# Projections in pairs of blocks by seven products of sums, one attention over all heads with operands through DRAM, and an output projection in two parts

## The chip, the cores and the metric

The kernel runs on one core of a Trainium2 chip. The metric is the device time of one execution in microseconds; lower is better. A core has TensorE (PE, the matrix engine, with its weight loads as PEld), VectorE (DVE), ScalarE (ACT), GpSimd (POOL) and SyncE (SP, which here issues nearly all DMAs). Each engine, and each engine's DMA queue, takes its own instructions in order; semaphores order the engines among each other. SBUF is the on-chip memory with 128 partitions, PSUM the accumulators of TensorE, DRAM the device memory.

## The reference

One layer of a hybrid backbone. The latent x is 1024 tokens (a grid of 16 rows of 64 columns) by 1024 features, the context 256 tokens by 1024. Both are normalised and modulated to h; one projection w_in (1024 x 3840) feeds a short convolution, an attention over 8 heads of 64 features, and a Conformer convolution; each result is gated, and one output projection is added to x.

```python
PROJ_SIZES = [W_SC] * 4 + [W_NA] * 4 + [W_CF] * 3      # 4 x 256, 4 x 512, 3 x 256 columns
...
def short_conv_branch(z_h, z_b, z_c, z_g, w_conv):
    return z_b * dwconv(z_c * z_h, w_conv) * jax.nn.silu(z_g)
...
def conformer_branch(z_p, z_q, z_g, w_conv, b_conv, ln_g, ln_b):
    u = z_p * jax.nn.sigmoid(z_q)
    u = dwconv(u, w_conv) + b_conv.astype(u.dtype)
    u = layernorm(u, ln_g, ln_b)
    return jax.nn.silu(u) * jax.nn.silu(z_g)
...
    s_win = jnp.einsum('bqhd,brqchd->bhqrc', qr, kw).astype(jnp.float32) * scale + bias[None]
    s_ctx = jnp.einsum('bqhd,bkhd->bhqk', qr, kc).astype(jnp.float32) * scale
    s = jnp.concatenate([s_win.reshape(b, h, GRID_W, kr * NA_COLS), s_ctx], axis=-1)
    p = jax.nn.softmax(s, axis=-1).astype(v.dtype)
```

A query of the attention sees a window of 8 rows by 16 columns of the grid, with a learned bias, and all 256 context keys. The Conformer's convolution has 31 taps on 256 channels, the short one 3 taps.

## The kernel before, in words

**Arithmetic.** A float32 product is made of two parts each, hi and lo (fp32r): three matmuls, h_hi·w_hi, h_lo·w_hi and h_hi·w_lo, which `mm_k` (L324 to L326) issues for one k of 128 input features. `split` (L129, L130) makes the parts: ACT copies, and VectorE or GpSimd subtracts. h lies in SBUF with features on partitions, in `h_lat` (hi and lo, 8 k by 1024 tokens) and `h_ctx`.

**Projection.** w_in is 30 blocks of 128 columns. A block's weights come by two DMAs (`wr`, two buffers) and are split, the low part on GpSimd. 26 blocks give features on partitions: for each half of 512 tokens 8 k by three matmuls into one PSUM buffer of `ps_z` (three buffers), which a sink then reads. The values' four blocks are projected together with tokens on partitions by `v_proj`, 10 tiles of 128 tokens by 8 k by three (L412 to L414), and stored to DRAM (`vd`). The keys of the context add 8 k by three matmuls of 256 columns per pair of heads.

**Stages.** `start` norms x and the context, computes the modulation and projects the first pair's queries and keys; its order is written out in the table SEQ for VectorE, ACT, GpSimd and SP. Then come `cf_in(0)`, the context keys of pair 0, `v_proj`, and the gate of pair 0. Four times `attend` runs a pair of heads: 16 blocks of 128 queries, and between them 48 units of projection (one unit is one k, three matmuls) from an iterator of what is left (`MF`, three units a block). An attention block is `scores` (PE into the one buffer of `ps_s`; VectorE adds the bias and takes the minimum, ACT exponentiates, GpSimd scales), two blocks later `transposed` (PE into the one buffer of `ps_t`; ACT and VectorE split), then `values` into `po` and `fold`. Queries come through `qd` DMAs out of SBUF (`q_parts`, L359), values through `vt` from DRAM (`v_load`, L435), the bias tables of the next head by 21 DMAs (L502). After attention the output projection `out_mm` (8 tiles of tokens by 2 halves by 8 channels by 3) runs as a stage of its own, with the gate multiplied on VectorE (`out_part`).

**Order.** On PE the program's own order holds. Helpers keep a clock of PE work (`pe`), and `spawn`, `poll` and `yield` insert the other coroutines by it: the 62 operations of the 31-tap convolution (L685, 1024 columns on VectorE), `ada_gates`, the bias set-up. Behind the start stage a scheduler orders the other engines, so their instructions stand where their inputs let them.

Of the kernel before, what the change touches and what calls it, by code (L numbers as in the profile page):

```python
# [16 lines left out]
P = 128  # L17
# [20 lines left out]
MF = (3, 3, 3, 3)  # L38
# [3 lines left out]
R_CF, R_CFB, R_LNG, R_LNB, R_SC = 0, 62, 64, 66, 68  # L42

# [13 lines left out]
b4 B30 m4 g4 v4 b5 B31 g5 v5 R3 m5 C3 n4 a6 f6 u6 a7 f7 u7 q80 n5 b6 g6 v6 q90 m6 b7 g7 v7 r82 m7 x8 n6 x9  # L57
O Q00 c0 c1 h0 o0 h1 o1 Q01 n7 c2 c3 h2 o2 h3 o3 Q02 Q10 Q11 Q12
# [7 lines left out]
class Builder:  # L66
# [237 lines left out]
    def load_w(self, src):  # L304
        return [w for g in range(2) for w in self.split_w(self.load_wraw(src, g))]
# [7 lines left out]
    def split_w(self, wr):  # L313
# [3 lines left out]
        self.split(wh, wl, wr, self.nc.gpsimd)  # L317
        return [(wh[:, i], wl[:, i]) for i in range(hk)]
# [27 lines left out]
    def sink_q(self, half, ps):  # L346
# [4 lines left out]
        hi, lo = (self.qn[:, i].rearrange("p b (r c) -> p r b c", c=BW)[:, rows] for i in range(2))  # L351
# [3 lines left out]
    def q_parts(self, h, bg):  # L355

        q = self.qp.tile([P, 2, 4, P], F32R, name="qd")
        for d in range(2):
            self.nc.sync.dma_start(out=f32(q[64 * d:64 * d + 64]),  # L359
                                   in_=f32(self.qn[64 * h:64 * h + 64, :, 4 * bg:4 * bg + 4]))  # L360
# [13 lines left out]

    def sink_gate(self, half, ps):
        sl = slice(half * HALF, (half + 1) * HALF)
        self.silu2(self.sg[:, sl], ps)
# [9 lines left out]
    def v_weights(self, pool):  # L387
        self.wv = wh, wl = [pool.tile([P, KT, HALF], F32R, name=f"wv{i}") for i in range(2)]
        raw = [self.t4.tile([P, T], F32, name="acc") for _ in range(2)]
        raw.append(self.t4.tile([P, T + NTAP - 1], F32, name="t4", tag="t4")[:, 0:T])  # L390
        raw.append(self.t2.tile([P, T], F32, name="yb", bufs=1))
        k = 0
        todo = []
        for t in raw:
            n = t.shape[1] // HALF
            t = t.rearrange("p (k n) -> p k n", n=HALF)
            src = self.a["w_in"][k * P:(k + n) * P, 2048:2048 + HALF].rearrange("(k p) n -> p k n", p=P)
            self.nc.sync.dma_start(out=t, in_=src)
# [793 lines left out]
```

## Time and profile before

| what | us |
|---|---|
| runs of the kernel before | 617.97 and 619.17, median 618.57 |
| the profiled execution's own time | 617.89 |
| its span in the trace | 616.1 |
| TensorE busy in it | 593.8 |
| VectorE, ACT, GpSimd busy | 401.1, 244.0, 178.4 |

In the profile a row of a group is: line of the kernel, engine, operation, output tile <- input tiles, shapes, number of instructions, then busy time and mean duration in ns, then the idle time before them and what ended it. A row of the timeline begins with start and duration in us. A row of the windows has, for a stretch of the span, the busy time and number of instructions of each engine, the clock granted to TensorE, the share of time in which the DMA engines were busy, and their rate. SPq rows are DMAs as SP issues them.

### The profile page before, as it was taken

The numbers are of one execution on the slowest core, as the hardware profiler recorded it, in microseconds if no ns is written. First come the engines' busy times: TensorE is split into PE (matmuls) and PEld (weight loads), VectorE is DVE, ScalarE is ACT, GpSimd is POOL, SyncE is SP. The second block draws the span as 40 slices with busy tenths as digits, with TensorE's granted clock in tenths as the row PEclk, the third lists the DMA queues.
The fourth block names the chain that finished last, engine by engine and source line by source line (L and its number), as shares of the span: only waits on it lengthen the run. The fifth ranks groups of instructions, "written<-read, shape, count | busy, mean of one in ns | idle before, by whom it ended". The sixth has DMA issues, their size and how long they took to land.

```text
span 616.1 us, 8935 instructions
## 1 busy us (share of the span) xinstructions
PE 593.8 (96%) x3101; PEld 497.0 (81%) x3101; DVE 401.1 (65%) x682; ACT 244.0 (40%) x468; POOL 178.4 (29%) x199
## 2 busy tenths in 40 slices
PE   7799999899999999999999999999999999999995
PEld 5467887688888888888888888888788888888884
DVE  4466977798356589577797666836879456352433
ACT  2455812111255542455523554424645434331222
POOL 1231112300233221424322433313434270265112
PEclk9999999899999999999999999999999999999998
DMA  8991658965623117331146242172311455770122
GB/s 286 357 326 41 222 151 175 158 173 160 164 49 93 37 55 202 75 86 49 28 136 141 48 113 55 36 222 52 82 28 35 133 151 160 273 272 1 70 102 103
DMA packets 97171, 78.64 MB, mean 128 GB/s; under 512 B 26508, under 2 KB 80870, under 8 KB 96998
## 3 DMA queue, kind: packets, MB, share of 16 engines
q1 hardware_dynamic: 95397, 71.51, 41.6%
q10 hardware_dynamic: 1728, 6.55, 3.0%
q8 instruction: 25, 0.41, 0.3%
q14 instruction: 21, 0.16, 0.1%
HBM read 55.93 MB, written 14.29 MB: 114 GB/s over the span
## 4 chain that ended last, share of the span: by engine, by line
PE 82%; DVE 6%; DMA 4%; ACT 2%; issue 2%; SPq 1%; POOL 1%; DVEq 0%; POOLq 0%; ACTq 0%
PE ps_z L324 13%; PE ps_z L326 13%; PE ps_z L325 13%; PE po L620 5%; PE ps_t L608 5%; PE ps_f L868 5%; PE ps_f L869 5%; PE ps_f L867 5%; PE ps_s L589 4%; DMA t<-in_w_ada 2%; PE ps_s L590 2%; PE ps_z L412 2%; PE ps_z L414 2%; PE ps_z L413 2%; DMA wa<-in_w_ada 2%
## 5 line engine op out<-in xcount | busy, mean ns | idle before, releaser
L324 PE MATMUL ps_z<-h,wh 128*128 128x512 f32 x384 | 151.1, 394 | 0.0
L326 PE MATMUL ps_z<-h,wl 128*128 128x512 f32 x384 | 150.2, 391 | 0.0
L325 PE MATMUL ps_z<-h,wh 128*128 128x512 f32 x384 | 149.7, 390 | 0.0
L130 POOL TENSOR_TENSOR wl<-wr,wh 128x512 fp32r<-128x512 f32 x52 | 71.8, 1384 | 146.8 <-ACT wh L129 118.0
L599 POOL TENSOR_SCALAR pr<-pr,sm 128x640 f32<-128x640 f32 (+1 forms) x64 | 52.9, 827 | 138.0 <-DVE sm L598 117.2
L326 PEld LDWEIGHTS ps_z<-h,wl 128*128 128x128 f32 x384 | 72.1, 188 | 16.1
L685 DVE SCALAR_TENSOR_TENSOR acc<-t,half_w,acc 128x1024 f32<-128x1024 f32 x60 | 83.0, 1384 | 1.0
L325 PEld LDWEIGHTS ps_z<-h,wh 128*128 128x128 f32 x384 | 72.2, 188 | 12.4
L324 PEld LDWEIGHTS ps_z<-h,wh 128*128 128x128 f32 x384 | 72.2, 188 | 12.1
L612 ACT ACTIVATE pw<-ps_t 128x640 fp32r<-128x640 f32 (+1 forms) x64 | 43.5, 680 | 90.7 <-PE ps_t L608 90.6
L594 DVE CUSTOM_DVE_ANT_0 ps_s<-ps_s,bt 128x640 f32<-128x640 f32 (+1 forms) x64 | 51.0, 796 | 33.7 <-PE ps_s L590 31.0
L613 DVE TENSOR_TENSOR pw<-ps_t,pw 128x640 fp32r<-128x640 f32 (+1 forms) x64 | 50.4, 788 | 17.3 <-ACT pw L612 16.9
L597 ACT ACTIVATE pr<-ps_s,mn 128x640 f32<-128x640 f32 (+1 forms) x64 | 49.0, 766 | 20.2 <-DVE mn L594 19.2
L620 PE MATMUL po<-pw,vt 128*128 128x256 f32 x304 | 51.3, 297 | 2.0 <-DVE yb L571 1.0
L868 PE MATMUL ps_f<-wol,y 128*128 128x512 f32 (+1 forms) x136 | 51.6, 379 | 0.0
L869 PE MATMUL ps_f<-woh,y 128*128 128x512 f32 (+1 forms) x136 | 51.5, 379 | 0.0
L867 PE MATMUL ps_f<-woh,y 128*128 128x512 f32 (+1 forms) x136 | 51.5, 379 | 0.0
L129 ACT ACTIVATE wh<-wr 128x512 fp32r<-128x512 f32 x52 | 32.5, 629 | 34.9 <-PE ps_z L325 20.9
L608 PE MATMUL ps_t<-ident,pr 128*128 128x128 f32 x304 | 43.6, 272 | 0.0
L620 PEld LDWEIGHTS po<-pw,vt 128*128 128x128 f32 x304 | 40.4, 189 | 3.8 <-issue 3.4
L589 PE MATMUL ps_s<-kt,qd 128*128 128x384 f32 (+1 forms) x128 | 42.2, 351 | 0.5 <-ACT pr L597 0.4
L608 PEld LDWEIGHTS ps_t<-ident,pr 128*128 128x128 f32 x304 | 36.0, 142 | 1.8 <-issue 0.9
(171 smaller groups left out, 911.4 us busy)
## 6 DMA issues: line engine op xcount, KB each, us to landing
wr<-in_w_in SPq DMA_DIRECT2D x52, 256.0 KB
wa<-in_w_ada SPq DMA_DIRECT2D x16, 512.0 KB
qd<-qn SPq DMA_DIRECT2D x32, 256.0 KB
vd<-t SPq DMA_DIRECT2D x20, 256.0 KB
x_in<-in_x SPq DMA_DIRECT2D x8, 512.0 KB
t<-in_w_ada SPq DMA_DIRECT2D x16, 256.0 KB
vt<-vd SPq DMA_DIRECT2D x32, 128.0 KB
fraw<-in_w_out SPq DMA_DIRECT2D x8, 512.0 KB
```

Source lines behind the costliest of these rows:

```text
L130: i2 = (eng or nc.vector).tensor_tensor(out=lo, in0=src, in1=f32(hi), op=ALU.subtract)
L324: nc.tensor.matmul(ps, lhsT=wh, rhs=hh, start=(k == 0), stop=False)
L325: nc.tensor.matmul(ps, lhsT=wh, rhs=hl, start=False, stop=False)
L326: self.last = nc.tensor.matmul(ps, lhsT=wl, rhs=hh, start=False, stop=(k == KT - 1))
L589: nc.tensor.matmul(win, lhsT=q[:, b % 4], rhs=kwin, start=(i == 0), stop=(i == 1))
L599: nc.gpsimd.tensor_scalar(out=pr, in0=pr, scalar1=sm, scalar2=0.5, op0=ALU.mult, op1=ALU.mult)
L608: nc.tensor.transpose(out=pt[:, c * P:(c + 1) * P], in_=pr[:, c * P:(c + 1) * P], identity=self.ident)
L620: self.nc.tensor.matmul(po, lhsT=vt[:, vi, h], rhs=pw[:, c], start=(c == 0), stop=(c == n - 1))
L685: self.after_pe(nc.vector.scalar_tensor_tensor(out=acc, in0=u[:, t:t + T], scalar=self.half_w[:, 2 * t + ct:2 * t + ct + 1], in1=acc, op0= ...
L867: nc.tensor.matmul(ps, lhsT=yh, rhs=wh[:, ch], start=(first and i == 0), stop=False)
L868: nc.tensor.matmul(ps, lhsT=yh, rhs=wl[:, ch], start=False, stop=False)
L869: nc.tensor.matmul(ps, lhsT=yl, rhs=wh[:, ch], start=False, stop=(last and i == len(chs) - 1))
```

## The change

1. **Start.** The start stage projects the queries of pairs 0 and 1 (before: queries and keys of pair 0) and stores them to DRAM (`Q`, `Z`). It also loads and splits the first context keys' weights (`Y`, `y`).
2. **Context keys.** `k_ctx` projects the context keys of all four pairs in a row, 96 matmuls of 256 columns, and stores them.
3. **Values and half-sums.** `v_proj` takes its tiles in the order 4 to 7, then 0 to 3, 8, 9. Meanwhile `t_first` and `t_last` build the three sums and one difference of quarters of h that the seven products need (tokens in halves, input features in halves); one quarter is stored to DRAM, overwritten, and loaded again afterwards (`block12`).
4. **Seven products.** `sum_products` projects ten pairs of blocks. Two blocks by two halves of the input features form a 2 x 2 matrix of weights, and two halves of tokens by two halves of features one of h; the 2 x 2 product is made of seven products of sums (the Winograd form of Strassen's) instead of eight: 7 x 4 k x 3 matmuls. `sum_weights` builds the sums of weights on GpSimd and VectorE and splits all seven, six low parts on GpSimd. The results are put together with `snap` (ACT, PSUM to SBUF), `add` (VectorE, onto PSUM) and one addition on GpSimd. The 31-tap convolution runs beside this (`conv_all`, from the third pair on).
5. **Attention in one piece.** `attention` runs over all 64 blocks of eight heads; keys, values, queries and gates are loaded per head from DRAM (`kv_load`, `q_parts`). Between two blocks stand two units of other work: first the last two pairs of blocks in the old form (gates of pairs 2 and 3, the Conformer's gate), then `out_first`, the output projection's part of the convolution channels (0, 1, 6, 7), which adds x and stores the sum to DRAM (`xr`).
6. **Output.** The attention channels (2 to 5) follow after attention, onto `xr`. The gate is multiplied into w_out on GpSimd (`load_wout`) rather than into the results.

The diff, cut to its core:

```diff
-O Q00 c0 c1 h0 o0 h1 o1 Q01 n7 c2 c3 h2 o2 h3 o3 Q02 Q10 Q11 Q12
+O Q00 c0 c1 h0 o0 h1 o1 Q01 n7 c2 c3 y0 h2 o2 h3 o3 y1 Q10 Q11 Z
...
+    def k_ctx(self, w0):
...
+        ws, raw = [w0, split(raws(1))], raws(2)
+        for pair in range(NPAIR):
+            yield from self.proj(ws[pair], T, TC, lambda ps: sink(pair, ps))
+            if pair < 2:
+                ws.append(split(raw))
+                if pair == 0:
+                    raw = raws(3)
...
+    def kv_load(self, hd):
+        pair, h = hd // 2, hd % 2
+        kt = self.slot(h, TA)
+        self.nc.sync.dma_start(out=f32(kt), in_=self.kd_dram[pair][:, h])
+        vt = self.slot(2 + h, (NB + 2) * P).rearrange("p (n e) -> p n e", e=P)
...
+        for b in range(NB):
+            src = bass.AP(tensor=vd.tensor, offset=vd.offset + b * BW * D + c, ap=[[GW * D, 16], [D, BW], [1, P]])
+            dma(out=f32(vt[:, b]), in_=src)
...
+    def sum_weights(self, cols):
...
+        for c0, c1, f in cols:
+            a11, a21, a22 = raw(c0, 0, f), raw(c1, 0, f), raw(c1, 1, f)
+            yield parts(a11)
+            s1 = op(G, a21, a22, ALU.add)
+            s3 = op(V, a11, a21, ALU.subtract, a21)
+            yield parts(s3)
+            s2 = op(G, s1, a11, ALU.subtract)
+            a12 = raw(c0, 1, f)
+            yield parts(s2)
+            yield parts(a12)
+            s4 = op(V, a12, s2, ALU.subtract, s2)
+            yield parts(s1)
+            yield parts(s4, V)
+            yield parts(a22)
...
+            for m in (1, 7, 6, 2, 5, 3, 4):
+                wh, wl = todo.popleft()
+                todo.extend(itertools.islice(ws, 1))
+                chain = m in (1, 6, 5)
+                ps = s if chain else self.ps_z.tile([P, HALF], F32, name="ps_z", tag="z")
+                for i in range(KT // 2):
...
+                if m == 1:
+                    s1 = snap(s)
+                elif m == 7:
+                    s7 = snap(ps)
+                elif m == 6:
+                    s2 = snap(s)
+                    nc.gpsimd.tensor_tensor(out=s2, in0=s2, in1=s7, op=ALU.add)
+                elif m == 2:
+                    add(ps, s1)
+                    sink(0, 0, ps)
+                elif m == 5:
+                    s4 = snap(s)
+                    add(s, s7)
+                    sink(1, 1, s)
+                elif m == 3:
+                    add(ps, s4)
+                    sink(0, 1, ps)
+                else:
+                    add(ps, s2, ALU.subtract)
+                    sink(1, 0, ps)
...
+                self.spawn(self.conv_all(2.1))
...
+                if b == 4 and hd < 7:
+                    kv[hd + 1] = self.kv_load(hd + 1)
...
+        next(steps)
+        while go(fill, 2):
+            next(steps)
...
+            nc.gpsimd.tensor_tensor(out=raw, in0=raw, in1=self.gates[half].unsqueeze(1).to_broadcast([P, 2, HALF]),
+                                    op=ALU.mult)
```

How the order moves, at three places. The first is TensorE at the end of the start stage. In the names, `ps_z` is a PSUM buffer, `h_78` and `h_79` (after: `hc_106`, `hc_107`) the hi and lo parts of h of the latent (after: of the context). Before:

```order
L1012 MATMUL po<-h_79,wh 128x512
L279 MATMUL ps_h<-ident,x_in 128x128 x8
L146 MATMUL ps_a<-ident,rows 128x74
L324 MATMUL ps_z<-h_78,wh 128x512
L325 MATMUL ps_z<-h_79,wh 128x512
L326 MATMUL ps_z<-h_78,wl 128x512
```

After:

```order
L1201 MATMUL po<-h_100,wh 128x512
L280 MATMUL ps_h<-ident,x_in 128x128 x8
L147 MATMUL ps_a<-ident,rows 128x74
L325 MATMUL ps_z<-hc_106,wh 128x256
L326 MATMUL ps_z<-hc_107,wh 128x256
L327 MATMUL ps_z<-hc_106,wl 128x256
```

The start stage is followed by the context keys' 256-column matmuls, 24 for each pair's weights, where a block of 512-column matmuls stood.

The second is VectorE beside the convolution (`acc`). Before, in `v_proj`, it alternates with the split of the values (`t`):

```order
L424 TENSOR_TENSOR t_1149<-ps_z,t_1149 128x4x64
L685 SCALAR_TENSOR_TENSOR acc<-t_734,half_w,acc 128x1024
L424 TENSOR_TENSOR t_1153<-ps_z,t_1153 128x4x64
L685 SCALAR_TENSOR_TENSOR acc<-t_734,half_w,acc 128x1024 x2
L424 TENSOR_TENSOR t_1187<-ps_z,t_1187 128x4x64
```

After, in a job of seven products, with sums of weights (`wq`), a low part (`wl`), the adds onto PSUM (`ps_z`, `ps_s`) and the sink of queries or keys (`st_hcb`):

```order
L377 TENSOR_TENSOR st_hcb<-ps_z,st_hcb 64x8x8x8
L524 TENSOR_TENSOR wq<-wq 128x512
L872 SCALAR_TENSOR_TENSOR acc<-t_1403,half_w,acc 128x1024
L131 TENSOR_TENSOR wl<-wq,wh 128x512
L872 SCALAR_TENSOR_TENSOR acc<-t_1403,half_w,acc 128x1024
L524 TENSOR_TENSOR wq<-wq 128x512
L872 SCALAR_TENSOR_TENSOR acc<-t_1403,half_w,acc 128x1024
L564 TENSOR_TENSOR ps_z<-snap,ps_z 128x512
L872 SCALAR_TENSOR_TENSOR acc<-t_1403,half_w,acc 128x1024 x2
L564 TENSOR_TENSOR ps_s<-snap,ps_s 128x512
L564 TENSOR_TENSOR ps_z<-snap,ps_z 128x512
```

The adds, which free PSUM for TensorE, stand behind one or two convolution steps each. GpSimd in the same jobs, where before it had only the low parts of weights, after:

```order
L586 TENSOR_TENSOR snap<-snap 128x512
L131 TENSOR_TENSOR wl<-wq,wh 128x512 x2
L524 TENSOR_TENSOR wq<-wq 128x512
L131 TENSOR_TENSOR wl<-wq,wh 128x512 x3
L524 TENSOR_TENSOR wq<-wq 128x512
```

It has nine operations of 512 columns per job: six low parts, two sums of weights and one sum of results.

The third is SP's queue in attention. Before, around the end of a pair (`wr` weights, `vt` values, `yd` a store of results, `qd` queries, `bt` bias tables):

```order
L310 DMA wr<-in_w_in 128x4x128 x2
L435 DMA vt<-vd 128x1x256 x8
L437 DMA vt<-vd 128x2x256
L556 DMA yd_61<-yb 128x1024
L359 DMA qd<-qn 64x2x512 x4
L310 DMA wr<-in_w_in 128x4x128 x4
L502 DMA bt_1122<-u_960 24x1x64
L502 DMA bt_1122<-u_960 72x1x128
L502 DMA bt_1122<-u_960 32x1x64
```

After, in the middle of a head (`sl` are the slots of queries, keys and values, `sgd` a store of gates):

```order
L361 DMA sl_3997<-qd_71 64x2x512 x2
L604 DMA sgd_83<-t_3952 128x512
L311 DMA wr<-in_w_in 128x4x128 x2
L442 DMA sl_4107<-kd_77 128x1280
L707 DMA bt_2363<-u_1567 24x1x64
L707 DMA bt_2363<-u_1567 72x1x128
L707 DMA bt_2363<-u_1567 32x1x64
L707 DMA bt_2363<-u_1598 24x1x64
L707 DMA bt_2363<-u_1598 72x1x128
L707 DMA bt_2363<-u_1598 32x1x64
L447 DMA sl_4109<-vd 128x1x128 x4
L772 DMA yd_61<-yb 128x1024
```

Each head has loads of its own for keys and values, and the store of a pair's result stands between them.

More of the change, by code (lines that the diff above doesn't have):

```diff
@@ L36 @@
 UROWS = 39
-MF = (3, 3, 3, 3)
 LAG = 2
@@ new lines, in t_all, with t_last @@
+    def t_all(self):
+        yield from self.t_first()
+        while not self.b12_read:
+            yield 1.0
+        yield from self.t_last()
+    def t_last(self):
+        nc = self.nc
+        self.block12(True)
+        for i in range(KT // 2):
+            t, u = (self.wq.tile([P, HALF], F32, name="wq", tag="wq") for _ in range(2))
+            for o, part in ((t, 0), (u, 1)):
+                nc.gpsimd.tensor_tensor(out=o, in0=f32(self.t_op[6][part][:, i]),
+                                        in1=f32(self.hsel(part, KT // 2 + i, 0, HALF)), op=ALU.subtract)
+            nc.gpsimd.tensor_tensor(out=t, in0=t, in1=u, op=ALU.add)
+            self.split(self.hh(i, HALF, HALF), self.hl(i, HALF, HALF), t)
+            yield 2.5
@@ L688, in cf_conv, with conv_all @@
                 yield 1
-    def conv_part(self, n, gap):
-        for _ in range(n):
-            if next(self.conv, 0) == 0:
-                return
+    def conv_all(self, gap):
+        for _ in self.cf_conv():
             yield gap
+        yield from self.cf_norm()
     def cf_norm(self):
@@ L830, in gate_rows @@
-    def gate_rows(self, pool):
+            self.split(*hl, acc[:, cs])
+            g = self.t2.tile([P, HALF], F32, name="t2", tag="t2")
+            nc.sync.dma_start(out=g[0:1], in_=self.a["b_ada"][:, 2 * D + cs.start:2 * D + cs.stop])
+            yield 4.0
+            ps = self.ps_z.tile([P, HALF], F32, name="ps_z", tag="z")
+            for j in range(2):
+                nc.tensor.matmul(ps, lhsT=self.ones_r, rhs=hl[j], start=(j == 0), stop=(j == 1))
+            nc.vector.tensor_tensor(out=g[0:1], in0=ps[0:1], in1=g[0:1], op=ALU.add)
@@ L832, in gate_rows, with load_wout @@
+    def load_wout(self, half, chs, eng):
         nc = self.nc
+        w = [self.wo.tile([P, 4, HALF], F32R, name=f"wo{half}{i}", tag=f"wo{half}{i}") for i in range(2)]
         for i in range(2):
-            ps = pool.tile([P, HALF], F32, name="ps_g")
-            for j in range(2):
-                nc.tensor.matmul(ps, lhsT=self.ones_r, rhs=self.ghl[:, i, j], start=(j == 0), stop=(j == 1))
-            g = self.gate[:, i * HALF:(i + 1) * HALF]
-            nc.vector.tensor_tensor(out=g, in0=ps, in1=g, op=ALU.add)
@@ new lines, in build, with go, pair @@
+        self.ps_s = q(self.pool("ps_s", 1, PSUM, side="left"))
+        self.ps_t = q(self.pool("ps_t", 1, PSUM, side="left"))
+        self.pp = r(self.pool("pp", 2, side="right"))
+        self.ya = r(self.pool("ya", 1, side="right"))
+        steps = self.attention()
+        self.gate_rows()
+        def go(fill, n):
+            for _ in range(n):
+                if next(fill, None) is None:
+                    return False
+                self.poll()
+            return True
+        def pair(c0, c1, sink):
+            ws = [self.load_w(self.a["w_in"][:, c:c + P]) for c in (c0, c1)]
+            for half in range(2):
+                for i, w in enumerate(ws):
+                    yield from self.proj(w, half * HALF, HALF, lambda ps: sink(i, half, ps))
@@ new lines, in build @@
+        self.w_conv = [self.load_wout(0, self.conv_ch, nc.vector)]
+        for ch in self.conv_ch[2:]:
+            self.load_y(ch)
+        self.w_conv.append(self.load_wout(1, self.conv_ch, nc.gpsimd))
+        for _ in range(4):
+            next(steps)
+        fill = self.out_first()
+        k, loads = 0, {6: 2, 14: 3, 22: 4}
+        while next(steps, None) is not None:
+            go(fill, 2)
+            if k in loads:
+                self.load_y(loads[k])
+            k += 1
+        go(fill, 100)
```

727 lines of the change are left out of this document (415 added, 312 removed).

## The prediction, made before the changed kernel was run

> **What bounds the kernel now.** I read the page's busy line, the slices and the chain of waits first; then the groups of instructions, the timeline of TensorE (PE) and the windows.
>
> ```profile
> span 616.1 us, 8935 instructions
> PE 593.8 (96%) x3101; PEld 497.0 (81%) x3101; DVE 401.1 (65%) x682; ACT 244.0 (40%) x468; POOL 178.4 (29%) x199
> ...
> PE   7799999899999999999999999999999999999995
> ...
> DVE  4466977798356589577797666836879456352433
> ...
> PEclk9999999899999999999999999999999999999998
> ...
> PE 82%; DVE 6%; DMA 4%; ACT 2%; issue 2%; SPq 1%; POOL 1%; DVEq 0%; POOLq 0%; ACTq 0%
> ...
> L324 PE MATMUL ps_z<-h,wh 128*128 128x512 f32 x384 | 151.1, 394 | 0.0
> ...
> L130 POOL TENSOR_TENSOR wl<-wr,wh 128x512 fp32r<-128x512 f32 x52 | 71.8, 1384 | 146.8 <-ACT wh L129 118.0
> ...
> L685 DVE SCALAR_TENSOR_TENSOR acc<-t,half_w,acc 128x1024 f32<-128x1024 f32 x60 | 83.0, 1384 | 1.0
> ```
>
> TensorE is busy for 96% of the span, is 82% of the chain and keeps its clock; only 22.3 us (616.1 - 593.8) are left without a matmul. So a matmul taken out is worth its issue period, as long as what feeds TensorE keeps up. The mean duration of 394 ns overlaps with the next matmul; the period is read from the timeline, whose columns are start, duration, engine:
>
> ```profile
> 83.77 0.39 PE L324 MATMUL ps_z<-h,wh 128*128 128x512 f32 x1
> ...
> 84.45 0.39 PE L324 MATMUL ps_z<-h,wh 128*128 128x512 f32 x1
> ```
>
> One L324, L325, L326 group takes 84.45 - 83.77 = 0.68 us: 0.2267 us a matmul of 512 columns.
>
> [...]
>
> **Term 1, the seven products.** Ten pairs of blocks each took 2 x 2 halves x 8 k x 3 = 96 matmuls; seven products of 4 k x 3 take 84. That is 10 x 12 = 120 fewer, 120 x 0.2267 = **-27.2 us**. Splitting the context keys out changes no columns, and attention's scores, transposes and values keep theirs: nothing there.
>
> **Term 2, what seven products cost the other engines.** Jobs 3 to 10 of the ten run beside the convolution; on TensorE they last 8 x 84 x 0.2267 = 152.3 us. The question is whether VectorE (DVE) and GpSimd (POOL) fit into that. Two rows show that they don't run freely side by side; the others give periods:
>
> ```profile
> 106.97 0.68 DVE L130 TENSOR_TENSOR t<-acc,t 128x512 fp32r<-128x512 f32 x1
> 107.58 0.41 DVE L424 TENSOR_TENSOR t<-ps_z,t 128x256 fp32r<-128x256 f32 x1
> 107.91 1.27 DVE L685 SCALAR_TENSOR_TENSOR acc<-t,half_w,acc 128x1024 f32<-128x1024 f32 x1
> 109.11 0.41 DVE L424 TENSOR_TENSOR t<-ps_z,t 128x256 fp32r<-128x256 f32 x1
> ...
> 230.79 2.29 DVE L685 SCALAR_TENSOR_TENSOR acc<-t,half_w,acc 128x1024 f32<-128x1024 f32 x1
> 230.71 1.29 POOL L130 TENSOR_TENSOR wl<-wr,wh 128x512 fp32r<-128x512 f32 x1 [8.22 <-ACT wh L129]
> ```
>
> A convolution step has a period of 109.11 - 107.91 = 1.20 us, a 512-column operation 107.58 - 106.97 = 0.61. Where a POOL subtraction had begun 0.08 us earlier, the step took 2.29 instead of 1.27: it did its work only after POOL's 1.29 us, so an operation that reads two SBUF operands and a POOL operation take turns; 1.02 + 0.08 = 1.10 us is what POOL holds, and 230.79 + 2.29 - 232.00 = 1.08 what the step does.
>
> The order of instructions gives for jobs 3 to 10 on DVE 54 convolution steps (64.8 us), 36 operations from SBUF alone (22.0), 68 with a PSUM operand (41.5) and about 3.5 of small ones, 131.8 in all; on POOL 72 additions and subtractions, 72 x 1.10 = 79.2. With no overlap at all: 211.0, 58.7 over TensorE. What could overlap with POOL is the PSUM operations, and 0.12 us of start of each step (54 x 0.12 = 6.5): 48.0. With all of it covered 163.0 are left, 10.7 over. I take four fifths covered, 211.0 - 38.4 = 172.6: **+20 us** (ends 0 and 59; 0 since POOL's splits can in part fall beside DVE's waits). The row nearest to this load is a stretch of before where DVE is almost full and TensorE still is:
>
> ```profile
> core 0: us, PE busy (x) PEld busy (x) DVE busy (x) ACT busy (x) POOL busy (x), PEclk, DMA share, GB/s
> 163.10:248.50 85.40, 85.21 (x481) 74.39 (x480) 60.68 (x104) 38.66 (x78) 25.59 (x27) 1.00 0.35 87
> 110.00:115.00 5.00, 5.00 (x16) 3.93 (x15) 4.96 (x6) 0.39 (x1) 0.32 (x1) 0.66 0.93 156
> 220.00:240.00 20.00, 20.00 (x101) 16.81 (x99) 18.67 (x19) 5.65 (x11) 5.05 (x4) 1.00 0.44 126
> 440.00:460.00 20.00, 18.27 (x117) 15.97 (x116) 15.74 (x42) 9.46 (x19) 6.85 (x10) 1.00 0.26 59
> ```
>
> In 220:240 POOL had 5.05 us of 20; in the jobs it has half of the time. And now results wait behind the convolution: each product's chain (snap on ACT, add on DVE, sink) must end before its PSUM buffer is used again, and a step that POOL delays holds up the adds queued behind it. Hence a loss rather than nothing. Snaps (ACT is 40% busy) and the stores of q, k and gates lie beside matmuls: nothing. If that cover goes, what is late is the add behind a snap, and with it the buffer of a product. The half-sums of h are built during the values' projection, 10 x 24 x 0.2267 = 54.4 us on PE, on a POOL that needs about 24 x 1.10 = 26; the convolution has left that stage, so nothing.
>
> **Term 3, attention in one piece.** In 163.10:248.50 one old pair of heads ran with its fill:
>
> ```profile
> L324 PE MATMUL ps_z<-h,wh 128*128 128x512 f32 x80 | 31.5, 394 | 0.0
> L324 PE MATMUL ps_z<-hc,wh 128*128 128x256 f32 x8 | 2.2, 280 | 0.0
> ...
> 200.73 11.38 SPq L502 DMA_DIRECT2D bt<-u  x15
> ...
> 172.47 1.36 SPq L359 DMA_DIRECT2D qd<-qn  x2
> ...
> 228.14 5.07 SPq L435 DMA_DIRECT2D vt<-vd  x8
> 233.25 0.59 SPq L437 DMA_DIRECT2D vt<-vd  x1
> 233.94 0.42 SPq L556 DMA_DIRECT2D yd<-yb  x1
> ```
>
> 80 fill units of 0.68 and 8 of 0.34 are 57.1 us of the 85.4, so a block of attention costs TensorE 28.3 / 16 = 1.77 us. After, a step is one block and two units, 1.77 + 1.36 = 3.13, and a head of eight 25.0; before, a head had 42.7 (85.4 / 2). SP must issue as many bias loads per head as before, and more of the rest: 21 x 0.76 (11.38 / 15) = 15.9; 8 value loads x 0.63 = 5.1; context values and the keys at 0.59 each, 1.2; 4 query loads x 0.68 = 2.7: 24.9 us of every 25.0. About 43 more issues (weights, gates, y, x and its sums) x 0.4 = 17. Seven heads: 7 x 24.9 + 17 = 191.6 against 7 x 25.0 = 175: 16 short. Queued behind each bias load are the query and value loads of the next head; TensorE waits for those. Some of it goes ahead of need in the first head; I take **+15 us** (ends 0, if the issue is shorter where the queue is not crowded, and 35, if TensorE waits at each head's start as well).
>
> **Term 4, the context keys.** Before, 24 matmuls of 256 columns followed each pair's other 192 products; now all 96 stand in a row, 2.7 us a pair, with weights through two buffers. The nearest load:
>
> ```profile
> 98.52 0.97 SPq L310 DMA_DIRECT2D wr<-in_w_in  x2
> ...
> 101.92 0.63 ACT L129 ACTIVATE wh<-wr 128x512 fp32r<-128x512 f32 x1 [2.56 <-DMA wr<-in_w_in]
> 103.16 0.63 ACT L129 ACTIVATE wh<-wr 128x512 fp32r<-128x512 f32 x1 [0.61 <-DMA wr<-in_w_in]
> ...
> 109.66 0.47 PE L412 MATMUL ps_z<-wv,h 128*128 128x512 f32 x1 [3.11 <-DVE t L424]
> ...
> 111.20 0.63 PE L412 MATMUL ps_z<-wv,h 128*128 128x512 f32 x1
> 111.62 0.63 PE L413 MATMUL ps_z<-wv,h 128*128 128x512 f32 x1
> ```
>
> From issue to ACT 3.4 and 4.6 us, then 0.63 and DVE's 0.61: 5 to 6 us a pair against 2.7, three times about 2.7: **+8 us**. Ends: 0 (loads far ahead) and 14: three gaps of 3.3, and a slow clock behind each. The 3.11 us without a matmul ahead of 109.66 are followed by matmuls 0.42 apart and a granted clock of 0.66 in 110:115, where 16 run instead of 22 (5.0 / 0.2267): 6 x 0.2267 = 1.4 us for each such gap.
>
> [...]
>
> **Output and end.** The output projection keeps its matmuls, in two parts; its first half fills attention. Gate multiplications of the weights go to POOL beside attention, the per-tile multiplication by the gate goes: nothing, ends -2 and +2.
>
> **Sum.** 616.1 - 27.2 + 20 + 15 + 8 = 631.9 us span. The profiled execution took 617.89, 1.8 outside its span: 633.7, **634 us**; the two runs shown are 617.97 and 619.17, median 618.57, 0.7 above that execution.
>
> **Rivals.**
> - *All covered* (ends faster): the engines' turns fall into gaps, SP's loads run ahead. 616.1 - 27.2 + 1.8 = 590.7 for nothing lost; with 10.7, the least that taking turns leaves, 601. For it: TensorE at 20.00 of 20 beside a DVE of 18.67. Against: POOL's half share, SP's 24.9 of 25.0. It decides, below 606.2, as long as terms 2 to 4 together stay under 15.5.
> - *One shortage binds*, the engines' turns or SP, not both: 590.7 + 15 or 20, with 0 to 8 of context keys: 606 to 619.
> - *The chain of attention binds too*: one score buffer (ps_s) must pass DVE, ACT before the next block's scores; a step shrinks from 42.7 / 8 = 5.3 to 3.13. 440:460, where normalisation shared DVE, lost 1.73 of 20 on PE. At 0.3 to 0.5 us a step, 64 steps cost 19 to 32 more: 653 to 666. Against: the pair in 163:248 lost 0.2 of 85.
>
> **How the numbers follow.** Terms 2 to 4 each partly binding: 0.42, own range 622 to 650. All covered: 0.23, 591 to 606. One shortage: 0.22. Attention's chain: 0.13. The range 598 to 658 leaves out the lower part of the second (0.08), the upper of the last (0.06) and the tails of the first (0.04). Two per cent of 618.57, about what can be told from no change, puts the bounds at 606.2 and 630.9. Faster: 0.23 and 0.01 of the third case, 0.24. Same: 0.21 of the third and 0.14 of the first below 630.9, 0.35. Slower: the rest, 0.41.
>
> **What would show it.** Right: 84 matmuls a job; jobs 3 to 10 near 172 us, with TensorE waiting for VectorE's adds or POOL's splits; SP busy without a break in attention, TensorE waiting for loaded keys, values or bias; gaps for weights in the context keys. Wrong: PE busy 97% or more between the start stage and the end (all covered), or waits for ps_s at each block (the chain). What would make the sum wrong most easily is term 2's covered share and whether SP's 0.76 us is the price of the issue itself or of a crowded queue.

## The result, and the profile after

The changed kernel takes 731.06 us (runs of 730.79 and 731.33) against 618.57 before: a ratio of 1.182, 95% interval 1.177 to 1.187. The forecast was 634 us with a range of 598 to 658; the sign was right, the size far too small. The span of the profiled execution went from 616.1 to 729.0 us, 112.9 more.

The page of the kernel after, the rows that answer to those shown of before:

```profile
span 729.0 us, 9323 instructions
PE 610.5 (84%) x2969; PEld 499.3 (68%) x2969; DVE 512.4 (70%) x792; ACT 301.1 (41%) x573; POOL 315.5 (43%) x278
...
PE   6898697999879989898877897989476789588994
...
DVE  3558699426579998999988778657873758267233
...
PEclk9999898999989999999989999999958999799998
...
DVE 27%; PE 26%; DMA 15%; SPq 10%; issue 9%; POOL 6%; ACT 6%; POOLq 0%; ACTq 0%; DVEq 0%
...
L131 POOL TENSOR_TENSOR wl<-wq,wh 128x512 fp32r<-128x512 f32 x60 | 91.6, 1532 | 75.9 <-ACT wh L130 53.4
L872 DVE SCALAR_TENSOR_TENSOR acc<-t,half_w,acc 128x1024 f32<-128x1024 f32 x60 | 101.0, 1683 | 0.4
```

TensorE was 82% of the chain of waits and is 26% of it now; 118.5 us (729.0 - 610.5) are without a matmul, where 22.3 were. No single engine took its place: VectorE, DMA and SP share the rest. The 60 convolution steps, the same work as before, take 101.0 us instead of 83.0: they are stretched.

The windows of the kernel after, one for each stage, from its first matmul to the next stage's (context keys, values, ten pairs, attention, output):

```profile
core 0: us, PE busy (x) PEld busy (x) DVE busy (x) ACT busy (x) POOL busy (x), PEclk, DMA share, GB/s
66.40:90.90 24.50, 16.23 (x96) 14.58 (x97) 18.87 (x33) 14.39 (x28) 11.50 (x7) 0.86 0.82 277
90.90:155.70 64.80, 59.17 (x242) 47.14 (x242) 45.66 (x52) 18.21 (x39) 38.19 (x26) 0.95 0.39 111
155.70:386.10 230.40, 205.98 (x845) 164.76 (x844) 198.06 (x199) 87.35 (x156) 137.21 (x100) 0.95 0.39 109
386.15:670.40 284.25, 224.65 (x1264) 193.87 (x1263) 193.48 (x403) 130.58 (x255) 92.65 (x90) 0.90 0.55 158
670.40:729.00 58.60, 48.21 (x223) 39.83 (x221) 20.59 (x34) 20.07 (x44) 23.86 (x35) 0.95 0.47 166
```

By the prediction's own periods TensorE needs 10.9 us for the context keys (96 x 0.1133), 54.4 for the values, 190.4 for the ten pairs (840 x 0.2267), 196.2 for attention with the 122 units of fill that run in it (64 x 1.77 + 122 x 0.68) and 47.6 for the output (198 x 0.2267 + 24 x 0.1133; the last six units of fill run there). So the stages lose 13.6, 10.4, 40, 88 and 11 us, 163 together. The kernel before took 551.0 us behind its start stage (from 65.1 on) for 27.2 us more of such work, 526.8, so by the same count it lost 24. The 112.9 us are then -27 for the matmuls, 163 - 24 = 139 for the losses, and 1.3 for a longer start stage.

The waits of TensorE in attention, in us in total, times, longest:

```profile
PE ps_s L809 <- DMA sl<-qd: 15.2, 4, 8.5
PE ps_s L809 <- ACT pr L817: 12.5, 12, 2.9
PE po L840 <- DVE yb L792: 9.8, 8, 2.7
PE ps_s L809 <- issue: 6.9, 1, 6.9
PE po L840 <- ACT wo L130: 3.4, 1, 3.4
```

Loads of queries lead; the chain of a block (`pr`, `yb`) follows in many small waits. The granted clock of 0.90 in this stage is a further loss: it was 0.50 in nine stretches, 58.0 of the 284 us together (the longest 525.53 to 546.01), and 1.00 in the rest.

### The profile page after: what moved, and what is told of

Read it like the earlier page. It is cut to its first block, busy times and chain, and to the rows that moved or that the text cites. A ratio compares the mean times of both kernels' runs of the same rounds, so it can differ in the third digit from the quotient of the medians.

```text
span 729.0 us, 9323 instructions
## 1 busy us (share of the span) xinstructions
PE 610.5 (84%) x2969; PEld 499.3 (68%) x2969; DVE 512.4 (70%) x792; ACT 301.1 (41%) x573; POOL 315.5 (43%) x278
## 4 chain that ended last, share of the span: by engine, by line
DVE 27%; PE 26%; DMA 15%; SPq 10%; issue 9%; POOL 6%; ACT 6%; POOLq 0%; ACTq 0%; DVEq 0%
DVE acc L872 7%; SPq L707 4%; DMA wq<-in_w_in 4%; PE ps_t L828 3%; PE po L840 3%; DMA sl<-qd 2%; PE ps_s L809 2%; DMA t<-in_w_ada 2%; DVE wq L524 2%; DMA sl<-kd 2%; PE ps_z L327 2%; PE ps_z L325 2%; PE ps_z L326 2%; DMA wr<-in_w_in 2%; DVE sl L131 1%
## 5 line engine op out<-in xcount | busy, mean ns | idle before, releaser
L131 POOL TENSOR_TENSOR wl<-wq,wh 128x512 fp32r<-128x512 f32 x60 | 91.6, 1532 | 75.9 <-ACT wh L130 53.4
L872 DVE SCALAR_TENSOR_TENSOR acc<-t,half_w,acc 128x1024 f32<-128x1024 f32 x60 | 101.0, 1683 | 0.4
L809 PE MATMUL ps_s<-sl,sl 128*128 128x384 f32 (+1 forms) x128 | 44.9, 370 | 37.8 <-DMA sl<-qd 15.2
L130 ACT ACTIVATE wh<-wq 128x512 fp32r<-128x512 f32 x70 | 43.5, 627 | 72.2 <-DVE wq L524 24.6
L840 PE MATMUL po<-pw,sl 128*128 128x256 f32 x304 | 56.9, 320 | 15.8 <-DVE yb L792 9.8
L817 ACT ACTIVATE pr<-ps_s,mn 128x640 f32<-128x640 f32 (+1 forms) x64 | 49.0, 766 | 31.4 <-PE ps_t L828 22.2
L809 PEld LDWEIGHTS ps_s<-sl,sl 128*128 128x128 f32 x128 | 26.5, 207 | 48.6 <-issue 27.8
L840 PEld LDWEIGHTS po<-pw,sl 128*128 128x128 f32 x304 | 44.9, 210 | 20.3 <-issue 7.8
L573 PE MATMUL ps_z<-h,wh 128*128 128x512 f32 x120 | 48.2, 402 | 3.7 <-DVE t L964 3.3
L573 PE MATMUL ps_s<-sl,wh 128*128 128x512 f32 x80 | 34.7, 433 | 16.2 <-ACT snap L560 16.2
L576 PE MATMUL ps_z<-h,wl 128*128 128x512 f32 x120 | 47.5, 396 | 0.0
L575 PE MATMUL ps_z<-h,wh 128*128 128x512 f32 x120 | 47.5, 396 | 0.0
L810 PE MATMUL ps_s<-sl,sl 128*128 128x256 f32 x128 | 37.9, 300 | 0.0
L524 POOL TENSOR_TENSOR wq<-wq 128x512 f32<-128x512 f32 x20 | 32.6, 1632 | 8.7 <-DMA wq<-in_w_in 4.6
L575 PE MATMUL ps_s<-sl,wh 128*128 128x512 f32 x80 | 33.5, 418 | 0.0
```

Source lines behind the costliest of these rows:

```text
L131: i2 = (eng or nc.vector).tensor_tensor(out=lo, in0=src, in1=f32(hi), op=ALU.subtract)
L524: eng.tensor_tensor(out=out, in0=a, in1=b, op=o)
L573: nc.tensor.matmul(ps, lhsT=wh[:, i], rhs=hh, start=(i == 0 and m not in (5, 6)), stop=False, skip_group_check=chain)
L575: nc.tensor.matmul(ps, lhsT=wh[:, i], rhs=hl, start=False, stop=False, skip_group_check=chain)
L809: nc.tensor.matmul(win, lhsT=q[:, b % 4], rhs=kwin, start=(i == 0), stop=(i == 1))
L817: nc.scalar.activation(out=pr, in_=s, func=AF.Exp, scale=-1.0, bias=mn, accum_out=sm)
```

## The experiments

All lengths of stages below are taken like the windows, from the first matmul of a stage to the first of the next. Where no interval is given, a time is that of one execution; 17 of the kernel before on one chip lay between 617.85 and 620.44, so differences above 3 us stand out.

| run | time, us | context keys | values | ten pairs | attention | output |
|---|---|---|---|---|---|---|
| changed kernel | 731.06 | 24.5 | 64.8 | 230.4 | 284.3 | 58.6 |
| bias_two_heads | 700.58 | 24.9 | 65.2 | 230.2 | 254.0 | 58.7 |
| no_taps | 703.25 | 24.8 | 65.5 | 207.9 | 277.5 | 60.0 |
| eight_products | 695.21 | 23.8 | 54.8 | 221.3 | 268.6 | 59.0 |
| eight_no_taps | 695.54 | 23.6 | 54.8 | 221.0 | 268.1 | 60.0 |
| ctx_weights_early | 731.86 | 14.5 | 74.7 | 229.7 | 286.8 | 58.7 |
| low_parts_on_dve | 725.04 | 24.0 | 65.3 | 226.4 | 282.8 | 58.7 |
| second_w_out_later | 726.49 | 24.6 | 65.5 | 230.8 | 278.4 | 58.6 |
| no_empty_steps | 731.05 | 24.5 | 65.6 | 231.3 | 286.6 | 54.5 |
| loads_by_act | 747.99 | 24.8 | 65.5 | 231.1 | 299.0 | 59.5 |
| eight_bias_ctx | 660.54 | 14.5 | 57.2 | 220.6 | 240.1 | 59.5 |
| eight_all_relief | 657.33 | 14.5 | 57.9 | 220.6 | 237.0 | 58.9 |

### Fewer bias loads

```diff
-                if b in (2, 4, 5) and hd < 7:
+                if b in (2, 4, 5) and hd < 1:
```

> The bias tables are loaded for heads 0 and 1 only and used again by the other heads: 126 of the 147 bias loads in attention are left out, some 93 us of SP's 196 us of issues there. Theory, SP's queue paces attention (issues, and loads that stand behind stores and loads that wait): the attention stage falls from 284 us to 215 to 235, the run to 662 to 682. Rival, the chain of one score buffer through VectorE, ScalarE and GpSimd paces it: the stage stays above 270, the run above 715.

The tables of heads 2 to 7 are left out; these heads use those of heads 0 and 1. The run fell by 30.5 us, all of it in attention (284.3 to 254.0). Heads 2, 3, 5 and 6 fell to 26.8, 26.5, 27.4 and 27.5 us (from 33.6, 27.7, 35.1 and 35.8), near TensorE's 25.0; the first two heads and head 4 (39.8) stayed long. So SP's queue is one cause, 30 us of the 88, and not the only one: the theory's 215 to 235 us was not reached, the rival's 270 neither.

How the queue does it is seen in the kernel after at the turn to the last head. Its rows on SP, from the load of keys to the next head's queries, and the TensorE row that waits:

```profile
609.68 0.47 SPq L442 DMA_DIRECT2D sl<-kd  x1
610.25 6.03 SPq L447 DMA_DIRECT2D sl<-vd  x8
616.32 0.59 SPq L448 DMA_DIRECT2D sl<-vd  x1
616.95 6.88 SPq L707 DMA_DIRECT2D bt<-u  x9
623.93 1.22 SPq L361 DMA_DIRECT2D sl<-qd  x2
...
629.25 0.55 PE L809 MATMUL ps_s<-sl,sl 128*128 128x256 f32 x1 [8.53 <-DMA sl<-qd]
```

The first queries are issued at 623.93, when TensorE has already stood still since 620.72 (629.25 - 8.53), and land five us later. They stand behind the value loads and nine bias loads of 0.76 us each (the middle table), which are needed from the head's second block on, one block later than the queries.

### The same loads, issued by ScalarE

```diff
-        self.nc.sync.dma_start(out=f32(kt), in_=self.kd_dram[pair][:, h])
+        self.nc.scalar.dma_start(out=f32(kt), in_=self.kd_dram[pair][:, h])
...
-        vd, c, dma = self.vd, hd * P, self.nc.sync.dma_start
+        vd, c, dma = self.vd, hd * P, self.nc.scalar.dma_start
...
-            self.nc.sync.dma_start(out=f32(q[64 * d:64 * d + 64]), in_=src[64 * h:64 * h + 64, :, 4 * bg:4 * bg + 4])
+            self.nc.scalar.dma_start(out=f32(q[64 * d:64 * d + 64]), in_=src[64 * h:64 * h + 64, :, 4 * bg:4 * bg + 4])
```

> In the changed kernel ScalarE issues the loads of keys, values and queries of each head (14 a head) instead of SP; the same loads with the same bytes, nothing left out. Theory, TensorE waits because these loads stand in SP's queue behind bias loads and behind stores that wait: heads 2, 3, 5, 6 fall by 3 to 8 us each, attention from 284 us to 250 to 268. Rival, the DMA engines' bandwidth or the number of transfers is short: attention stays above 278. Second rival, ScalarE pays for the issues (14 x 0.6 = 8 us a head) and delays its copies: attention gets longer than 284.

The second rival came true: attention took 299.0 us, longer than 284. The theory's figures did not: heads 2, 3, 5 and 6 took 31.4, 30.6, 34.2 and 33.7 us (before the edit 33.6, 27.7, 35.1 and 35.8). Its mechanism is still seen. TensorE's waits for loads are gone, and the last block of heads 0, 2, 5 and 6, in which they stood, falls from 6.8, 6.3, 6.9 and 12.6 us to 3.4, 3.3, 4.0 and 4.5. But the run is 17 us longer: the waits of TensorE in attention for ScalarE and for what depends on it have grown.

```profile
PE ps_s L809 <- ACT pr L817: 22.6, 15, 5.0
...
PE po L840 <- DVE yb L792: 16.8, 19, 2.7
PE ps_t L828 <- DVE pw L833: 14.4, 20, 1.4
PE ps_t L828 <- POOL pr L819: 11.9, 5, 5.0
```

The same transfers with the same bytes no longer hold TensorE up, so their place in a queue is what it waited for; and ScalarE, which is a link in the chain of each block, is the wrong queue for them. How much the edit would gain without ScalarE's part is not shown.

### The convolution left out, and eight products instead of seven

```diff
             for t in range(1, NTAP):
-                self.after_pe(nc.vector.scalar_tensor_tensor(
-                    out=acc, in0=u[:, t:t + T], scalar=self.half_w[:, 2 * t + ct:2 * t + ct + 1],
-                    in1=acc, op0=ALU.mult, op1=ALU.add))
                 yield 1
```

> 60 of the 62 operations of the 31-tap convolution are left out (the first tap of each channel half stays). Theory, VectorE and GpSimd taking turns holds up jobs 3 to 10 of the seven products: they fall from 188 us to 152 to 162, the run to 697 to 706. Rival, late weights or the chain from a product through the ACT snapshot: they stay above 175 us.

Jobs 3 to 10 fell from 188.2 to 164.8 us, the ten pairs to 207.9 against TensorE's 190.4: 2.8 us outside the theory's 152 to 162, far from the rival's 175; the run's 703.25 is inside its 697 to 706. Without the taps the ten pairs still take 17.5 us more than TensorE's work. Attention fell too, by 6.8 us; the last six taps of the changed kernel run in it:

```profile
408.64 1.27 DVE L872 SCALAR_TENSOR_TENSOR acc<-t,half_w,acc 128x1024 f32<-128x1024 f32 x1
```

This one, the last, begins 22 us into the stage; the normalisation of the convolution follows on VectorE (15.0 us of work) until 462.

The other edit keeps the taps and takes the sums away; `eight_products` runs each block as before:

```diff
-        self.run(self.sum_products(jobs))
+        self.run(self.eight_products(jobs))
...
-        self.spawn(self.t_all(), 14.0)
...
-        self.block12(False)
```

> The ten pairs of blocks are projected by eight products as before, without the half-sums of h and the sums of weights; all else as in the changed kernel. Theory, sums on VectorE and GpSimd cost more than the 120 matmuls save: the ten pairs take 218 to 226 us (960 x 0.2267 = 217.6) instead of 230, the values 55 to 58 instead of 65, the run 708 to 718. Rival, the seven products are still a gain and only what stands beside them is slow: the ten pairs take 245 us or more, the run 740 or more.

This is the largest step of all, 35.9 us: values 54.8 instead of 64.8, ten pairs 221.3 instead of 230.4 in spite of 120 more matmuls, and attention 268.6 instead of 284.3. The first two were expected, the last was not: the run came out 13 us below the theory's range. In this run all taps end before attention begins, and the normalisation ends 38 us into it instead of 76. Heads 0 to 2 are 9 us shorter together, head 4 is 7.6 shorter.

> Ten pairs by eight products, and 60 of the 62 operations of the 31-tap convolution left out: the fourth corner beside the changed kernel (ten pairs 230.4 us), seven products without taps (207.9) and eight with taps (221.2). Theory, the taps are dear only where the sums of the seven products fill VectorE and GpSimd: eight without taps take 217 to 220 us, so taps cost 22 us with seven products and 1 to 4 with eight. Rival, taps cost alike in both: eight without taps fall below 205 us, which TensorE's own 217.6 us excludes unless the period is shorter than 0.2267.

221.0 us for the ten pairs, one above the theory's 217 to 220, so the taps cost 22.5 us beside seven products (230.4 - 207.9) and 0.3 beside eight. The seven products save 13 us of the 27 when nothing stands beside them (221.0 - 207.9): sums of weights and putting together take the other 14. Of the 13, 10 are lost in the values' stage, where the half-sums are made; the convolution takes 22.5 more, so the change loses in all. Of attention's 16 us the taps account for 6.8 (284.3 to 277.5 with seven products) and for nothing with eight (268.6 and 268.1).

### Low parts on VectorE

```diff
-        def parts(t, eng=G):
+        def parts(t, eng=V):
```

> In the jobs of seven products all seven low parts of weights are made on VectorE instead of six on GpSimd; nothing is left out. Theory, the two engines take turns: a subtraction holds 1.10 us on GpSimd and 0.61 on VectorE, so 48 of them in jobs 3 to 10 moved over shorten the sum of both by 23 us although VectorE gets more to do; jobs 3 to 10 fall from 188 us to 165 to 178, the run to 705 to 720. Rival, the engines run independently and VectorE is simply overfull: it gets 48 x 0.61 = 29 us more, and jobs 3 to 10 take 195 us or more.

Jobs 3 to 10 took 182.1 us, 6.1 less, though VectorE, the fuller engine, got 48 operations more: the rival (195 or more) is out. The gain is smaller than the 10 to 23 of the theory, and the run's 725.04 lies above its 705 to 720. Turns taken with GpSimd are part of the loss; that a full VectorE is the rest is not shown by this run.

Beside a GpSimd operation, a subtraction of 512 columns takes 1.78 us instead of 0.68 in the kernel after (at 100.39, in the next experiment's rows) and a tap 2.33 instead of 1.27 (362.70, below). The 40 adds onto PSUM, 28 of them beside a GpSimd operation as well, take 0.68 to 0.70 us all the same.

The chain by which this reaches TensorE is seen in the timeline of the kernel after, in the last job:

```profile
362.66 3.49 POOL L131 TENSOR_TENSOR wl<-wq,wh 128x512 fp32r<-128x512 f32 x2 [3.58 <-ACT wh L130]
362.70 2.33 DVE L872 SCALAR_TENSOR_TENSOR acc<-t,half_w,acc 128x1024 f32<-128x1024 f32 x1
...
364.95 1.75 DVE L928 SCALAR_TENSOR_TENSOR t<-t,t 128x512 f32<-128x512 f32 x1
...
367.22 0.68 DVE L564 TENSOR_TENSOR ps_z<-snap,ps_z 128x512 f32<-128x512 f32 x1
...
368.00 0.60 ACT L610 ACTIVATE t<-ps_z 128x512 f32<-128x512 f32 x1 [4.41 <-DVE ps_z L564]
...
369.01 0.59 ACT L560 ACTIVATE snap<-ps_s 128x512 f32<-128x512 f32 x1
...
369.65 0.80 PE L573 MATMUL ps_s<-sl,wh 128*128 128x512 f32 x1 [5.99 <-ACT snap L560]
```

GpSimd's two low parts stretch a tap from 1.27 to 2.33 us and the next operation from 0.68 to 1.75; the add onto PSUM comes late; ScalarE waits 4.41 us with the gate's activation at the head of its queue, and the snapshot that TensorE needs stands behind it. TensorE, 5.99 us idle, then runs at half the clock (granted 0.50 in 369.65:375.30; 0.80 us for the first matmul and 0.63 for those behind it, instead of 0.39). In the ten pairs it waits 16.2 us for this snapshot, in six waits.

### Context keys' weights ahead

```diff
-        ws, raw = [w0, split(raws(1))], raws(2)
+        rr = {p: raws(p) for p in (1, 2, 3)}
+        ws = [w0, split(rr[1])]
```

`raws` here fills tiles of the pool `wq`, which holds eight.

> The context keys' weights of pairs 1 to 3 are loaded ahead into six buffers of another pool instead of passing through two. Theory, the weights' way from DRAM through two buffers makes the context keys take 24.5 us instead of 10.9: they fall to 12 to 15 us, the run to 719 to 722. Rival, VectorE's order (splits of the values' weights among the keys' splits and sinks) makes it: the stage stays above 20 us, or the values start as late as before.

The context keys fell by 10.0 us as the theory has it, and the total did not move: the values took 9.9 us longer. TensorE waited there 5.8 us for the low parts of the values' own weights (`wv`, made on VectorE) and 5.7 for the splits of the values; in the changed kernel only for the latter, 5.6. In that stage VectorE also makes half-sums, and takes turns with GpSimd's; that this holds up `wv` is argued, not shown. Rows of that stage in the kernel after:

```profile
98.08 1.79 DVE L131 TENSOR_TENSOR sl<-wq,sl 128x512 fp32r<-128x512 f32 x1
99.79 0.68 DVE L470 TENSOR_TENSOR wq<-wq 128x512 f32<-128x512 f32 x1
100.39 1.78 DVE L131 TENSOR_TENSOR sl<-wq,sl 128x512 fp32r<-128x512 f32 x1
...
99.95 1.68 POOL L461 TENSOR_TENSOR wq<-h,h 128x512 f32<-128x512 f32 x1 [0.63 <-DVE sl L131]
```

Operations of 0.68 us take 1.78 while GpSimd adds: 1.10 more, just what GpSimd was reckoned to hold. Without the half-sums the same edit pays: in the next run context keys and values take 71.7 us, in eight_products 78.6.

### Three reliefs at once

The edits of eight_products, bias_two_heads and ctx_weights_early in one kernel.

> Three edits in one: ten pairs by eight products, bias tables loaded for heads 0 and 1 only (126 loads left out), context keys' weights ahead. If their costs are separate, 731.1 - 35.9 - 30.5 and, with no half-sums behind the context keys, 10 less: 653 to 660. If they hide one another (a gain in one stage is lost again in the next), 670 or more. Attention then is what is left: 230 to 240 us against 200 of TensorE's work, with the switch at head 4 at 35 us or more.

660.54 us, 0.5 above the range for separate costs, with the context keys at 14.5 and the values at 57.2: the three costs are separate within 6 us (731.1 - 35.9 - 30.5 - 10 = 654.7). Attention is left with 240.1. Eight products give the 27 us of saved matmuls back, so what is left above the kernel before, 42 us, is all loss.

### The switch at head 4

At the end of the first fill, h is given up, and the memory is used for y and w_out; four steps of attention run without fill. Head 4 takes 46.1 us for some 20 of work (25.0, less four steps' fill of 1.36).

```diff
-        self.w_conv.append(self.load_wout(1, self.conv_ch, nc.gpsimd))
...
+                if half == 0 and tt == 2:
+                    self.w_conv.append(self.load_wout(1, chs, nc.gpsimd))
```

> The second half of the output projection's convolution weights is loaded, multiplied by the gate and split only after two tiles of the first half, instead of ahead of all of them; nothing is left out. Theory, the steps of attention without fill at the switch of head 4 are long because ScalarE, VectorE and GpSimd do the copies, multiplications and splits of y and w_out there: head 4 falls from 46 us to 36 to 42, the run to 722 to 728. Rival, the steps are long because the chain of one block alone lasts that long, or because of SP: head 4 stays within 3 us.

Head 4 fell to 40.5 us, the run by 4.6: as the theory says. The next edit comes on top of this one:

```diff
-        for _ in range(4):
-            next(steps)
         fill = self.out_first()
```

> The kernel of the run with the second half of w_out later, and without the four steps of attention that have no fill at the switch of head 4: the output projection's units follow at once and TensorE waits for their weights. Nothing is left out. Theory, the switch costs what it takes to bring y and w_out through DMA, GpSimd and the splits, whatever attention does meanwhile: head 4 and the total stay within 4 us of 724.7 of span. Rival, the four steps themselves are slow because without fill nothing covers the chain of a block: the total falls by 8 us or more.

The span is 729.3 instead of 724.7, 0.6 us outside the theory's 4 and on the other side from the rival. (The six last units of fill move from the output stage into attention, hence its 54.5.) The empty steps are not what costs; they use up a wait that is there anyway: DMA, GpSimd's multiplication by the gate and the splits. In the run with fewer bias loads, where SP is not in the way, the rows at the switch read:

```profile
530.24 4.69 POOL L1024 TENSOR_TENSOR t<-t,bt 128x1024 f32<-128x1024 f32 x2 [4.78 <-DMA t<-in_w_out]
534.88 2.39 POOL L131 TENSOR_TENSOR wo<-t,wo 128x1024 fp32r<-128x1024 f32 x1
...
532.64 1.06 ACT L130 ACTIVATE wo<-t 128x1024 fp32r<-128x1024 f32 x1 [3.00 <-POOL t L1024]
...
535.93 0.78 ACT L817 ACTIVATE pr<-ps_s,mn 128x640 f32<-128x640 f32 x1
...
536.85 0.69 PE L809 MATMUL ps_s<-sl,sl 128*128 128x384 f32 x1 [3.58 <-ACT pr L817]
```

ScalarE's copies of w_out wait for GpSimd's 4.69 us with attention's exponential (`pr`) behind them, and TensorE waits for that.

### All reliefs

The three edits, the second half of w_out later, and `hd < 0` in the condition of the bias loads.

> The run with three edits (658.8 us of span), with the bias loads of head 1 left out too (147 left out; all heads use the empty tables or head 0's) and the second half of the convolution part of w_out later. Theory, the first head is slow (32.9 us) because head 1's bias tables are issued in it: it falls to 26 to 29, head 4 from 39.5 to 32 to 35, the run to 645 to 652. Rival, the first head is slow because of the start of attention itself (empty chain, loads that could not be issued earlier): it stays above 31.

657.33 us, above the theory's 645 to 652. Head 0 fell only from 32.9 to 31.8 us: the rival holds, the start of attention is slow for another reason than bias loads. Head 4 fell from 39.5 to 36.7, not to 32 to 35. Attention at 237.0 is still 41 above TensorE's work: some 17 at the switch, 7 in head 0, and 9 in the last head (34.3 us), whose last block takes 10.8 while the chain runs out with no block behind it. The last two were not tried alone.

### The kernel before, improved

The gap of 3.1 us in the values' projection of the kernel before stands where the four stores of `ada_gates` hold all four small buffers (`t2`), which the values' splits use too:

```diff
                 nc.sync.dma_start(out=self.gd[:, h, n], in_=f32(hl[n]))
+            if h == 0:
+                yield 8.0
```

> The kernel before with one edit: 8 us of TensorE's work between the two halves of the gate's split, so that its stores hold two of the four small buffers at a time and not all four while the values' splits want them. Theory, this removes the gap of 3.1 us in the values' projection and the half clock behind it: 614 to 616.5 us against 618.6. Rival, the gap comes from the convolution's steps ahead of the splits on VectorE: no change.

616.22 us against 618.89, a ratio of 0.9967 (0.9953 to 0.9982): inside the theory's 614 to 616.5, a small gain. The 3.1 us wait is not there any more; one of 2.1 stands 11 us later. The granted clock was 1.00 in 100:120, where the kernel before had 0.66 in 110:115, and 0.998 over the run. This is the fastest kernel of the study.

> The same edit, and the convolution's steps in the values' stage 2.1 us of TensorE's work apart instead of 1.6 (25 there instead of 31, the rest in the later pairs). If the steps on VectorE cause the gap: 613 to 616 us; if the later pairs have no room for six more steps: 619 or more.

624.71 us, 1.009 (1.0075 to 1.0104), as the second alternative has it. TensorE falls 6 us behind between 229 and 344, where the two later rows of steps, now longer, run. A wait of 3.3 us is back in the values' stage, though the gate's halves are apart and the steps as well: what causes that gap is not settled by the two runs.

## Why the prediction was wrong, point by point

**Bound and term 1.** Right: 0.2267 us per matmul holds (eight products without taps take 221.0 us for 960 matmuls, 217.6 by the period), and 120 of them went.

**Term 2, +20 us: right in kind, too small.** Jobs 3 to 10 took 188.2 us, 36 over TensorE's work. "Four fifths covered" was the step that failed: 172.6 forecast. The turns of VectorE and GpSimd were right (low_parts_on_dve), and the taps were the part that did not fit (22.5 us). The late add was foreseen, its way to TensorE was not: the prediction has it hold a product's PSUM buffer, the trace has it hold ScalarE's queue, and so the snapshot behind it (16.2 us of waits). Also, the prediction counted 54 of the 60 convolution steps in these jobs and put nothing for the other six and the normalisation, which fall into attention.

**Half-sums, nothing: wrong.** They cost 10.0 us (64.8 against 54.8; the first sums of weights, at the end of the stage, are in that difference too). GpSimd's 26 us in 54 were taken as hidden, though the prediction's own row had shown VectorE stretched by a GpSimd operation (2.29 us for a tap instead of 1.27); the splits of the values stand behind these. Nearly all of the loss comes from two waits for such a split, 2.46 and 2.55 us, and a granted clock of 0.50 for 3.4 us behind each (115.93:119.34, 126.17:129.58).

**Term 4, +8 us: near.** 13.6, inside the ends of 0 and 14, though not as three gaps of 3.3: one wait of 4.70, 3.4 us lost to a granted clock of 0.50 behind it (81.80:88.62), and several short waits. Alone it would have been worth nothing to mend, because the values' stage was next.

**Term 3, +15 us: the main miss.** Attention lost 88. SP's issues were forecast at 191.6 us and measured at 198.1, and a bias load at 0.76 against 0.73 (107.5 us for 147). The step that failed was to compare the two sums, SP's 192 with TensorE's 175, as if the queue worked without a break: SP waited too (22.7 us in eight waits for the sums that it stores to `xr`), with other loads behind, and urgent ones stood behind loads not yet needed, while TensorE waited. The bias loads in the queue are worth 30 us (bias_two_heads). The rest was not in the list: the switch at head 4, which the diff shows as four steps without fill (26 us over its work; taking the second half of w_out away from there gave 6), a slow first head (9), a last head that took 41.0, and part of what the sums do, since eight products without any edit in attention made attention 16 us shorter. Of these 16 the six taps that run over into attention are worth 6.8. The other 9 stay open: they were not taken apart. What differs in the traces is the normalisation, which reaches 76 us into attention instead of 38, and head 4, 7.6 us shorter; the reload of a quarter of h falls away.

**Output, nothing: wrong by some 4.** The stage takes 58.6 us for 47.6 of work, 11 lost. TensorE waits for nothing there; the last matmul ends at 718.6, 10.4 us before the end, where the kernel before had 7.0 behind its last. It was not tested.

**Rivals.** The third, attention's chain, had 653 to 666 us; its waits exist (12.5 us on `pr`), but loads and the switch were more. None of the three reaches 731.

**The clock.** The slow clock behind gaps in the context keys was seen: behind a wait of 4.70 us (82.11) the first matmul of 256 columns took 0.58 us and most behind it 0.41, instead of 0.39 and 0.28 at full clock, and the stage's granted clock was 0.86. A gap of 4.70 is longer than the 3.3 that the prediction counted, so this row does not show it for those.

```profile
82.11 0.58 PE L325 MATMUL ps_z<-hc,wh 128*128 128x256 f32 x1 [4.70 <-ACT wh L130]
```

The values' stage does. Behind its waits of 2.46 us (ended at 115.55) and 2.55 us (at 125.43) the granted clock fell to 0.55 and 0.61 (the third number from the right):

```profile
115.60:119.00 3.40, 3.40 (x9) 2.70 (x10) 3.40 (x3) 0.00 (x0) 3.40 (x3) 0.55 0.27 80
125.40:129.00 3.60, 3.57 (x10) 2.87 (x11) 3.45 (x3) 1.18 (x3) 2.31 (x2) 0.61 0.93 246
```

So the prediction was right to count a slow clock behind gaps of up to 3.3 us. It is no sure thing either: behind waits of 2.64 and 2.73 us in attention (ended at 516.73 and 581.34) the granted clock stayed at 1.00 (in 516.73:525.50 and 581.34:593.80).

## What to carry to other kernels

Fewer matmuls are worth their period only where the engines that prepare and put together the products have room: here 27 us on TensorE were paid for with sums on two engines that take turns (0.68 us on VectorE became 1.78 beside GpSimd), beside a convolution that had been hidden until then. For a queue that issues in order, compare not the sums over a stage but the moment at which each urgent load is issued, and look what stands ahead of it. Where a stage hands memory over to the next, count the way of the new operands (transfer, multiplication, splits) as time without fill.

## What the runs showed of the hardware that was not expected

Beside GpSimd's additions, VectorE's 512-column operations on SBUF alone went from 0.68 to as much as 1.78 us each, and 60 taps from 83.0 to 101.0 us in total; moving work from GpSimd to the fuller VectorE made the stage 6 us shorter. Loads issued by ScalarE took 0.5 to 0.6 us each in loads_by_act (0.52 for queries at 425.04, 0.61 for values at 443.89), 17.4 us for 32 query loads and 39.8 for 64 value loads, about as on SP (medians of 0.58 and 0.60 in the kernel after). A wait of TensorE as short as 2.46 us was followed by 3.4 us at a granted clock of 0.50, one of 2.73 us by none.
